# Second products in seven block products, in two parts that are combined in place in PSUM

## The chip, the core and the metric

The program runs on one core of one Trainium2 chip. The time is device microseconds of one execution of the whole program. The kernel before takes 1732.32 us, the median of three runs (1731.59 to 1733.02).

## The reference

512 tokens of width 1024 go through two blocks, all in float32. What matters here are three products that end a feed-forward stage, each with the weight's rows as the dimension that is summed over:

```python
def swiglu(x, w_in, w_out):                       # in the first block, twice; w_out is 2816 x 1024
    gate, up = jnp.split(x @ w_in, 2, axis=-1)
    return (jax.nn.silu(gate) * up) @ w_out
# first_block, each of its two layers, behind differential or chunked attention:
    x = layer_norm(DEEPNORM_ALPHA * x + swiglu(x, ffn_w_in[l], ffn_w_out[l]), ln_g[l, 1], ln_b[l, 1])
# second_block, behind its mixer of spatial gating and gated linear attention; w_ff2 is 4096 x 1024:
    f = rmsnorm(h, pre_ff_g[l]) @ w_ff1[l]
    f = jnp.square(jax.nn.relu(f)) @ w_ff2[l]
    h = h + rmsnorm(f, post_ff_g[l])
```

The two `ffn` are called the first and the second ffn here; the product with `w_ff2` is the last product of the program.

## The kernel before

**A product in three passes.** Each float32 operand is split into a high part (`hi`, the value rounded to the matmul's type) and a low part (`lo`, the value minus `hi`). A product is the sum of hi by hi, hi by lo and lo by hi in PSUM, so each block of it costs three matmuls.

**Weights.** The class `Weights` brings the weights in, in the order of their use, as a list of units. A raw tile of 128 x 1024 (512 KB) is loaded from the SP queue into one of three buffers (`wraw`), or, for some, into a lent tile (`room`). ACT then copies it into `whi` (line 127), and DVE subtracts that from it into `wlo` (line 130). There are five buffers of such pairs, and a unit's split is issued when the unit five places ahead of it is released by its last matmul (`fill`, called by `done`). A raw buffer is loaded anew as soon as it has been read.

**First products.** The first product of an ffn (1024 by 5632) and of the last stage already goes, for most column pairs, by a seven-product scheme for two-by-two blocks (`Blocks`). It needs sums of weights on DVE (lines 104 to 113), and its PSUM banks are emptied by DVE additions (lines 530 to 535), followed by the product of gate and up (line 827). In this stage the SP queue loads 512 KB for a weight tile, and DVE does three or four kinds of work beside PE.

**Second products.** These are the three that change. `Out` is one such product, `out_phase` its loops. The activations h stand as tiles k of 128 rows (22 in an ffn, 32 in the last product), which are split when they are first used (lines 786 and 787, into `th`, `tl` or, in the last product, `sh`, `sl`). Eight PSUM banks hold the result: four token tiles t of 128 by two halves c of 512 columns. Per k and t six matmuls of 512 columns run (line 387):

```python
            for n, (a, b) in enumerate(((0, 0), (0, 1), (1, 0))):
                for c in halves:
                    nc.tensor.matmul(self.banks[t][c], act[a][:, ts(t)], w[b][:, 0, c * 512:(c + 1) * 512],
                                     start=first and n == 0, stop=last and n == 2)
```

One k for four t is thus 24 matmuls. All k but the last six, seven or four (the tail) run over all t; the tail then runs token tile by token tile, so that the normalisation behind it begins early. At places given by `SPARE` an ffn splits a unit further ahead into a free tile of h.

**Order.** The program is written as one stream, and a scheduler sets each engine's own order from the dependences and its estimate of times; the SP queue keeps the order in which loads are written. An engine works through its list in that order, so an instruction that waits holds up all behind it.

## Time and profile before

| | |
|---|---|
| median of three runs | 1732.32 us |
| profiled execution | 1732.78 us |
| its span | 1731.1 us |
| mean granted clock of TensorE over the span | 0.998 of full speed |
| PE busy | 1716.9 us, 99% |
| DVE busy | 1213.4 us, 70% |
| ACT busy | 874.1 us, 50% |
| POOL busy | 128.6 us, 7% |
| moved by DMA | 191.62 MB, mean 111 GB/s |

The span runs from the first to the last instruction; the execution's own time stands 1.7 us above it. Busy time is an engine's time inside instructions; PE's matmuls overlap, so that the time from one start to the next, and not the length of one, is what a matmul costs. The rows below come from the same execution.

### The profile page before, as it was taken

The numbers are of one execution on the slowest core, as the hardware profiler recorded it, in microseconds if no ns is written. First come the engines' busy times: TensorE is split into PE (matmuls) and PEld (weight loads), VectorE is DVE, ScalarE is ACT, GpSimd is POOL, SyncE is SP. The second block draws the span as 40 slices with busy tenths as digits, with TensorE's granted clock in tenths as the row PEclk, the third lists the DMA queues.
The fourth block names the chain that finished last, engine by engine and source line by source line (L and its number), as shares of the span: only waits on it lengthen the run. The fifth ranks groups of instructions, "written<-read, shape, count | busy, mean of one in ns | idle before, by whom it ended". The sixth has DMA issues, their size and how long they took to land.

```text
span 1731.1 us, 27660 instructions
## 1 busy us (share of the span) xinstructions
PE 1716.9 (99%) x10886; PEld 1539.1 (89%) x10886; DVE 1213.4 (70%) x2056; ACT 874.1 (50%) x1458; POOL 128.6 (7%) x237
## 2 busy tenths in 40 slices
PE   9999999999999999999999999999999999999998
PEld 9888889999988888888999999888877899988886
DVE  6988868999943666666889998446646588953333
ACT  6877635444533377776544445333525356642221
POOL 0312102000000111220000000001001100000000
PEclk9999999999999999999999999999999999999999
DMA  6644346343443255552334344331422224343331
GB/s 208 136 99 110 98 146 185 110 115 105 123 133 122 73 114 136 123 140 81 98 91 118 102 114 154 110 87 50 123 72 87 80 73 124 108 134 98 97 98 49
DMA packets 207203, 191.62 MB, mean 111 GB/s; under 512 B 8800, under 2 KB 176928, under 8 KB 207072
## 3 DMA queue, kind: packets, MB, share of 16 engines
q1 hardware_dynamic: 194384, 162.48, 32.0%
q0 software_dynamic: 12112, 25.52, 6.7%
q8 instruction: 86, 1.41, 0.3%
q10 hardware_dynamic: 576, 1.84, 0.3%
q14 instruction: 45, 0.37, 0.1%
HBM read 172.99 MB, written 7.38 MB: 104 GB/s over the span
## 4 chain that ended last, share of the span: by engine, by line
PE 90%; DVE 3%; issue 3%; ACT 2%; POOL 1%; DMA 0%; ACTq 0%; POOLq 0%; DVEq 0%
PE ps L297 53%; PE ps L387 30%; PE ps L928 1%; PE ps L916 1%; PE ps L315 1%; PE ps L598 1%; PE ps L599 1%; ACT x L643 1%; DVE wlo L130 0%; ACT whi L127 0%; PE ps L704 0%; PE ps L728 0%; POOL ln_st L292 0%; DMA kl<-low 0%; PE ps L1128 0%
## 5 line engine op out<-in xcount | busy, mean ns | idle before, releaser
L127 ACT ACTIVATE whi<-wraw 128x1024 fp32r<-128x1024 f32 (+2 forms) x338 | 339.5, 1007 | 294.6 <-PE ps L297 162.3
L130 DVE TENSOR_TENSOR wlo<-wraw,whi 128x1024 fp32r<-128x1024 f32 (+2 forms) x338 | 390.5, 1159 | 105.9 <-ACT whi L127 102.9
L297 PE MATMUL ps<-xh,whi 128*128 128x256 f32 (+1 forms) x1220 | 379.4, 312 | 0.3 <-ACT xh L317 0.3
L297 PE MATMUL ps<-xl,whi 128*128 128x256 f32 (+1 forms) x1220 | 377.7, 310 | 0.5 <-DVE xl L318 0.3
L297 PE MATMUL ps<-xh,wlo 128*128 128x256 f32 (+1 forms) x1220 | 377.5, 310 | 0.0
L297 PEld LDWEIGHTS ps<-xh,wlo 128*128 128x128 f32 x1220 | 232.5, 191 | 11.2
L297 PEld LDWEIGHTS ps<-xl,whi 128*128 128x128 f32 x1220 | 232.5, 191 | 10.7 <-DVE xl L318 0.9
L297 PEld LDWEIGHTS ps<-xh,whi 128*128 128x128 f32 x1220 | 232.0, 191 | 10.7 <-ACT xh L317 0.5
L297 PE MATMUL ps<-th,whi 128*128 128x256 f32 x784 | 217.5, 277 | 0.0
L297 PE MATMUL ps<-tl,whi 128*128 128x256 f32 x784 | 217.1, 277 | 0.0
L297 PE MATMUL ps<-th,wlo 128*128 128x256 f32 x784 | 216.7, 276 | 0.0
L297 PEld LDWEIGHTS ps<-th,whi 128*128 128x128 f32 x784 | 147.6, 188 | 0.1
L297 PEld LDWEIGHTS ps<-tl,whi 128*128 128x128 f32 x784 | 147.6, 188 | 0.1
L297 PEld LDWEIGHTS ps<-th,wlo 128*128 128x128 f32 x784 | 147.3, 188 | 0.0
L297 PE MATMUL ps<-whi,xh 128*128 128x256 f32 (+1 forms) x384 | 124.4, 324 | 0.0
L297 PE MATMUL ps<-whi,xl 128*128 128x256 f32 (+1 forms) x384 | 122.5, 319 | 0.0
L297 PE MATMUL ps<-wlo,xh 128*128 128x256 f32 (+1 forms) x384 | 122.5, 319 | 0.0
L387 PE MATMUL ps<-whi,th 128*128 128x512 f32 x312 | 96.5, 390 | 0.0
L387 PE MATMUL ps<-whi,tl 128*128 128x512 f32 x312 | 96.1, 389 | 0.0
L387 PE MATMUL ps<-wlo,th 128*128 128x512 f32 x312 | 96.0, 389 | 0.0
L292 POOL TENSOR_TENSOR ln_st<-rs_in,mhalf 128x1 f32<-128x1 f32 x39 | 27.4, 702 | 821.6 <-DVE rs_in L291 814.6
L787 DVE TENSOR_TENSOR tl<-h,th 128x512 fp32r<-128x512 f32 x44 | 29.9, 690 | 79.4 <-ACT th L786 79.4
(350 smaller groups left out, 3164.8 us busy)
## 6 DMA issues: line engine op xcount, KB each, us to landing
wraw<-in_ffn_w_in SPq DMA_DIRECT2D x73, 512.0 KB, 4.7
wraw<-in_w_ff SPq DMA_DIRECT2D x60, 512.0 KB, 4.0
wraw<-in_ffn_w_out SPq DMA_DIRECT2D x44, 512.0 KB, 3.7
wraw<-in_a_w_qkv SPq DMA_DIRECT2D x23, 512.0 KB, 4.9
wraw<-in_w_in SPq DMA_DIRECT2D x20, 512.0 KB, 3.7
wraw<-in_kv_w SPq DMA_DIRECT2D x16, 512.0 KB, 4.1
room<-in_ffn_w_in SPq DMA_DIRECT2D x15, 512.0 KB, 4.0
copies<-extd POOLq DMA_DIRECT2D x16, 320.0 KB, 8.6
```

The lines of the kernel that those rows point to most:

```text
L127: self.nc.scalar.activation(hi[:, sl], t[:, sl], AF.Copy)
L130: self.nc.vector.tensor_tensor(lo[:, sl], t[:, sl], hi[:, sl].bitcast(F32), op=OP.subtract)
L292: nc.gpsimd.tensor_tensor(r, u[:, :n], mhalf[:, :n], op=OP.pow)
L297: nc.tensor.matmul(ps, lhs[a][lsel], rhs[b][rsel], start=first and n == 0, stop=last and n == 2)
L315: nc.tensor.transpose(p[:, k, :], y[:, ts(4 * c + k)], ident)
L387: nc.tensor.matmul(self.banks[t][c], act[a][:, ts(t)], w[b][:, 0, c * 512:(c + 1) * 512], start=first and n == 0, stop=last and n == 2)
L598: yield lambda: nc.tensor.matmul(p[:, :N], part[m][:, ts(i)], part[2 + m][:, :N], start=True, stop=False)
L599: yield lambda: nc.tensor.matmul(p[:, :N], part[m][:, ts(i)], part[4 + m][:, :N], start=False, stop=True)
L643: nc.scalar.activation(qs[32 * g:32 * g + 32], p[32 * (g ^ 1):32 * (g ^ 1) + 32], AF.Copy)
L787: nc.vector.tensor_tensor(lo, src[k], hi.bitcast(F32), op=OP.subtract)
L916: nc.tensor.transpose(p[:, j], e[:, ts(j)], ident)
L928: nc.tensor.matmul(p[:, q0:], v, aT[q][:, kt, q0:], start=kt == 0 and q == 0, stop=kt == NT - 1 and q == 1)
```

## The change

The contracted tiles of a second product are taken in pairs q, as two-by-two blocks: the even tile of weights is (B11 B12), the odd one (B21 B22), each block 512 columns; the activations' blocks A11, A12 belong to the first 256 tokens and A21, A22 to the last 256. Seven block products take the place of eight, for the first eight pairs of each ffn (`TWOF`) and twelve pairs of the last product (`TWO`). Each block product is two token tiles in three passes, 6 matmuls of 512 columns, so a pair has 42 in place of 48.

With S1 = A21 + A22, S2 = S1 - A11, S3 = A11 - A21, S4 = A12 - S2 and T1 = B12 - B11, T2 = B22 - T1, T3 = B22 - B12, T4 = B21 - T2 (the code works with its negative where that saves an operation):

- First part, for all pairs of the product in turn: S1·T1, S2·T2 (weights of the unit a0), A11·B11, S3·T3 (unit a1). Each goes into its own two banks, over all pairs.
- Between the parts the eight banks are combined once. ACT copies the banks of A11·B11 and of S1·T1 to SBUF after the last A11; DVE then adds S2·T2 to the copy of A11·B11 (line 547 of the changed kernel), and, in place in PSUM, adds this sum to the bank of S1·T1 (line 555) and to that of S3·T3 (line 557), and the copy of S1·T1 to that, into the bank of S2·T2 (line 558).
- Second part, again for all pairs: A12·B21, S4·B22 (unit b0) and A22·T4 (unit b1), added to the banks. Before A22·T4 its banks must have gone through lines 557 and 558, before S4·B22 its bank through line 555. A22·T4 goes into one half of columns only, the first.

After the last pair of the second part the banks hold the plain product of all pairs. The remaining tiles (6 in an ffn, 8 in the last product) run as before. In the last product the order after the first part is: pairs 0 to 2, tiles 24 and 25, pairs 3 to 5, tiles 26 and 27, pairs 6 to 11, and tiles 28 to 31 as tail.

**Weights.** Both tiles of a pair are needed in both parts, so they are loaded twice; in the first part only B22 of the odd tile (256 KB). The odd tiles go into lent buffers: in an ffn two in turn (`e1`, which is a tile named `e1` or, in the second ffn, `y`, and `room`), in the last product three in turn (two `y` and half of `gb`). DVE forms T1, T2, T3 from the raw tiles (lines 103 to 105) or T4 (lines 112 to 114). The low part of some units is not DVE's any more: for them ACT writes the negative high part into `lo` (the raw tile times -1, rounded), and a DMA issued by POOL adds the raw tile to it; these are the `added` units, a0 of the pairs with q not divisible by 4, and b0 of the pairs with q = 1, 4, 7, 10. In all other units line 157 does what line 130 did.

**Activations.** They are summed for two pairs at a time (lines 503, 504, 505 and 511, of 512 columns each), and split on ACT and DVE (line 494) into `th`, `tl` for the first two pairs of an ffn, else into eight places of 512 columns in `xh`, `xl`, which hold the ffn's input until its first product ends.

The diff, cut to its core:

```diff
+TWO, TWOF = 12, 8
...
+        while self.loaded <= i + (part not in (None, 0, "b0")):
             self.load()
+        tt = self.nc.vector.tensor_tensor
+        if part in ("a0", "b1"):
+            (e0, e1), (o0, o1) = ((t[:, :512], t[:, 512:]) for t in (self.r[i + (part == "b1")], self.r[i + (part == "a0")]))
+        if part == "a0":
+            tt(o0, e1, e0, op=OP.subtract)
+            tt(e1, o1, e1, op=OP.subtract)
+            tt(o1, o1, o0, op=OP.subtract)
+            return self._used(i + 1)[:, :], None
+        if part == "a1":
+            return self._used(i)[:, :], None
+        if part == "b0":
+            return self.r[i][:, :], None
+        if part == "b1":
+            tt(e1, e1, e0, op=OP.subtract)
+            tt(e1, e1, o1, op=OP.subtract)
+            tt(e0, o0, e1, op=OP.add)
+            self._used(i)
+            return self._used(i + 1)[:, :512], None
         if part is None:
             return self._used(i)[:, :], None
         if part == 0:
...
                 self.nc.scalar.activation(hi[:, sl], t[:, sl], AF.Copy)
                 if between:
                     between()
+                if self.split in self.added:
+                    self.nc.scalar.activation(lo[:, sl], t[:, sl], AF.Copy, scale=-1.0)
+                    self.nc.gpsimd.dma_start(lo[:, sl], t[:, sl], accum_op=OP.add)
+                    continue
                 self.nc.vector.tensor_tensor(lo[:, sl], t[:, sl], hi[:, sl].bitcast(F32), op=OP.subtract)
...
+    def spec_two(key, w, q, kind, transfer, group):
+        for n in range(2):
+            at[key, kind, q, n] = len(units)
+            if n in transfer:
+                added.add(len(units))
+            units.append((len(specs), kind + str(n)))
+        for odd in (0, 1) if kind == "a" else (1, 0):
+            c = 512 if kind == "a" and odd else 0
+            if odd and (kind == "b" or q > 1):
+                lent[len(specs)] = group
+            specs.append((cols(w, 256 * q + 128 * odd, 1, c, 1024 - c), (1, 1024 - c), None, c))
     wqkv = ins["a_w_qkv"]
...
+        w = ins["ffn_w_out"][l]
+        for q in range(TWOF):
+            spec_two(("fo", l), w, q, "a", (0,) if q % 4 else (), 2 + l)
+        for q in range(TWOF):
+            spec_two(("fo", l), w, q, "b", (0,) if q % 3 == 1 else (), 2 + l)
+        for k in range(2 * TWOF, 22):
+            spec((("fo", l), k), w, 128 * k, 1, 0, D)
...
-    rows("f2", ins["w_ff2_2"], 32)
+    w = ins["w_ff2_2"]
+    for q in range(TWO):
+        spec_two("f2", w, q, "a", (0,) if q % 4 else (), 4)
+    second = []
+    for q in range(TWO):
+        second.append(("b", q))
+        spec_two("f2", w, q, "b", (0,) if q % 3 == 1 else (), 4)
+        if q % 3 == 2 and 2 * TWO + 2 * (q // 3) + 2 <= 28:
+            for k in range(2 * TWO + 2 * (q // 3), 2 * TWO + 2 * (q // 3) + 2):
+                second.append(("one", k))
+                spec(("f2", k), w, 128 * k, 1, 0, D)
+    tail_f2 = [k for k in range(2 * TWO, 32) if ("one", k) not in second]
+    for k in tail_f2:
+        spec(("f2", k), w, 128 * k, 1, 0, D)
...
+    def two_parts(o, key, n_two, second, view, slots, tmp, z5, side={}):
...
+        def split(b, name, v):
+            hi, lo = slots(b, name)
+            nc.scalar.activation(hi, v, AF.Copy)
+            tt(lo, v, hi.bitcast(F32), op=OP.subtract)
+            parts[b, name] = hi, lo
+        def blocks(b):
+            v = view(b)
+            return [v[:, :, tile, half] for half in range(2) for tile in range(2)]
+        def sums(b):
+            (a11, a12, a21, a22), (s1, s2) = blocks(b), tmp
+            tt(s1, a21, a22, op=OP.add)
+            tt(s2, s1, a11, op=OP.subtract)
+            tt(a21, a11, a21, op=OP.subtract)
+        def splits(b):
+            (a11, a12, a21, a22), (s1, s2) = blocks(b), tmp
+            for name, v in (("S1", s1), ("S2", s2), ("A11", a11), ("S3", a21)):
+                split(b, name, v)
+            tt(a11, a12, s2, op=OP.subtract)
+        def first(b):
+            sums(b)
+            splits(b)
+        def then(b):
+            a11, a12, a21, a22 = blocks(b)
+            split(b, "A12", a12)
+            split(b, "S4", a11)
+            split(b, "A22", a22)
+        def product(unit, half, q, name, t0, c, begin):
+            w, act = W.get(at[unit]), parts[q // 2, name]
+            for m in range(2):
+                for n, (i, j) in enumerate(((0, 0), (0, 1), (1, 0))):
+                    nc.tensor.matmul(o.banks[t0 + m][c], act[i][:, q % 2, ts(m)], w[j][:, 4 * half:4 * half + 4],
+                                     start=begin and n == 0, stop=False, skip_group_check=True)
+        u = [t.rearrange("p a b -> p (a b)") for t in tmp]
+        def part_a():
+            for t in range(NT):
+                o.banks[t] = [bank(), bank()]
+            for q in range(n_two):
+                if q % 2 == 0 and q + 2 < n_two:
+                    first(q // 2 + 1)
+                product((key, "a", q, 0), 0, q, "S1", 0, 1, q == 0)
+                product((key, "a", q, 0), 1, q, "S2", 2, 1, q == 0)
+                W.done(at[key, "a", q, 0])
+                product((key, "a", q, 1), 0, q, "A11", 0, 0, q == 0)
+                if q == n_two - 1:
+                    then(0)
+                    for m in range(2):
+                        nc.scalar.activation(z5[:, m], o.banks[m][1], AF.Copy)
+                        nc.scalar.activation(u[m], o.banks[m][0], AF.Copy)
+                        tt(u[m], o.banks[2 + m][1], u[m], op=OP.add)
+                product((key, "a", q, 1), 1, q, "S3", 2, 0, q == 0)
+                W.done(at[key, "a", q, 1])
+        yield lambda: sums(0)
+        yield lambda: splits(0)
+        part_a()
+        for m in range(2):
+            tt(o.banks[m][1], o.banks[m][1], u[m], op=OP.add)
+        for m in range(2):
+            tt(o.banks[2 + m][0], o.banks[2 + m][0], u[m], op=OP.add)
+            tt(o.banks[2 + m][1], o.banks[2 + m][0], z5[:, m], op=OP.add)
+        for kind, q in second:
+            for f in side.get(q, ()) if kind == "b" else ():
+                f()
+            if kind == "one":
+                for t in range(NT):
+                    o(q, t)
+                o.done(q)
+                continue
+            if q % 2 == 0 and q + 2 < n_two:
+                then(q // 2 + 1)
+            product((key, "b", q, 0), 0, q, "A12", 0, 0, False)
+            product((key, "b", q, 0), 1, q, "S4", 0, 1, False)
+            W.done(at[key, "b", q, 0])
+            product((key, "b", q, 1), 0, q, "A22", 2, 0, False)
+            W.done(at[key, "b", q, 1])
...
+                o = Out(("fo", l), range(2 * TWOF, 22), splitter(lambda k: at_t(k - 2 * TWOF, 16), h))
+                halves = lambda t: t.rearrange("p (q s) -> p q s", q=2)
+                extra, lend = [hp.tile([128, D], F32, name=f"e{n}", bufs=1) if l == 0 else yp_[0].tile([128, D], F32, name="y")
+                               for n in range(2)], []
+                def lender():
+                    lend.append((extra[1], room)[len(lend) % 2])
+                    return lend[-1]
+                W.lender[1 + l] = lender
+                turn = []
...
+                def slots(b, name):
+                    if b == 0 and name in ("S1", "S2", "A11", "S3"):
+                        return [halves(t) for t in at_t(("S1", "S2", "A11", "S3").index(name), 0)]
+                    turn.append(name)
+                    return [halves(t[:, len(turn) % 8]) for t in (xh, xl)]
...
+                two = two_parts(o, ("fo", l), TWOF, [("b", q) for q in range(TWOF)],
+                                lambda b: four[b].rearrange("p (q e f s) -> p q e f s", q=2, e=2, f=2), slots,
+                                [halves(extra[0][:, n * S:n * S + S]) for n in range(2)],
+                                four[5][:, 2 * S:].rearrange("p (a b) -> p a b", a=2),
+                                {0: [norm_parts], 5: [spare], 6: [spare], TWOF - 1: [inner]})
+                first_sums, first_parts = next(two), next(two)
...
+                side = side_steps(then, 0, 2)
+                side[39] = [first_sums]
+                in_tiles(keys, evac, 4, tails, fast, side)
+                for f in two:
+                    f()
+                out_phase(o, finish, after, 22 - 2 * TWOF)
```

On DVE, at the end of the first ffn's first product: in both kernels the last block of that product is emptied from `ps` into `gb` (four instructions), with other work between. Before:

```order
L530 TENSOR_TENSOR gb_100<-ps_5289,gb_100 128x2x256
L787 TENSOR_TENSOR tl_2796<-h4_2786,th_2795 128x512
L531 TENSOR_TENSOR gb_100<-ps_5290,gb_100 128x512
L130 TENSOR_TENSOR wlo_5404<-wraw_5309,whi_5403 128x1024
L532 TENSOR_TENSOR gb_100<-ps_5290,gb_100 128x256
L535 TENSOR_TENSOR gb_100<-ps_5291,gb_100 128x512
L787 TENSOR_TENSOR tl_2796<-h4_2786,th_2795 128x512
L787 TENSOR_TENSOR tl_2796<-h4_2787,th_2795 128x512
L827 TENSOR_TENSOR h4_2791<-gb_100 128x512
L787 TENSOR_TENSOR tl_2796<-h4_2787,th_2795 128x512 x2
L130 TENSOR_TENSOR wlo_5447<-wraw_5340,whi_5446 128x1024
```

After; here `e0` holds sums of activations, `e1` and `wraw` are the raw tiles of a pair, and h4 are the activations:

```order
L690 TENSOR_TENSOR gb_100<-ps_5297,gb_100 128x2x256
L103 TENSOR_TENSOR e1_2799<-wraw_5317 128x512
L691 TENSOR_TENSOR gb_100<-ps_5298,gb_100 128x512
L157 TENSOR_TENSOR wlo_5390<-wraw_5256,whi_5389 128x1024
L692 TENSOR_TENSOR gb_100<-ps_5298,gb_100 128x256
L104 TENSOR_TENSOR wraw_5317<-e1_2799,wraw_5317 128x512
L695 TENSOR_TENSOR gb_100<-ps_5299,gb_100 128x512
L105 TENSOR_TENSOR e1_2799<-e1_2799 128x512
L503 TENSOR_TENSOR e0_2798<-h4_2787 128x512
L1019 TENSOR_TENSOR h4_2791<-gb_100 128x512
L504 TENSOR_TENSOR e0_2798<-e0_2798,h4_2787 128x512
L505 TENSOR_TENSOR h4_2787<-h4_2787 128x2x256
```

Between the four instructions now stand the sums of weights and of the next two pairs' activations where splits of activations (line 787) stood.

On DVE, further on in the same product, where the changed kernel passes from the first to the second part. Before, only two kinds of instruction alternate there:

```order
L787 TENSOR_TENSOR tl_2796<-h4_2788,th_2795 128x512
L130 TENSOR_TENSOR wlo_5477<-wraw_5374,whi_5476 128x1024
L787 TENSOR_TENSOR tl_2796<-h4_2788,th_2795 128x512
L130 TENSOR_TENSOR wlo_5509<-wraw_5407,whi_5508 128x1024
L787 TENSOR_TENSOR tl_2796<-h4_2788,th_2795 128x512
L130 TENSOR_TENSOR wlo_5541<-wraw_5450,whi_5540 128x1024
L787 TENSOR_TENSOR tl_2796<-h4_2788,th_2795 128x512
L130 TENSOR_TENSOR wlo_5573<-wraw_5480,whi_5572 128x1024
```

After; `e0` holds the sums for the combination, a half of `h4` the copy of S1·T1, and `ps` are the banks:

```order
L547 TENSOR_TENSOR e0_2798<-ps_5439,e0_2798 128x512
L547 TENSOR_TENSOR e0_2798<-ps_5441,e0_2798 128x512
L555 TENSOR_TENSOR ps_5435<-ps_5435,e0_2798 128x512
L555 TENSOR_TENSOR ps_5437<-ps_5437,e0_2798 128x512
L112 TENSOR_TENSOR wraw_5670<-wraw_5670 128x512
L557 TENSOR_TENSOR ps_5438<-ps_5438,e0_2798 128x512
L113 TENSOR_TENSOR wraw_5670<-wraw_5670,room_2797 128x512
L558 TENSOR_TENSOR ps_5439<-ps_5438,h4_2791 128x512
L114 TENSOR_TENSOR wraw_5670<-room_2797,wraw_5670 128x512
L557 TENSOR_TENSOR ps_5440<-ps_5440,e0_2798 128x512
L494 TENSOR_TENSOR xl_81<-h4_2787,xh_80 128x512
L157 TENSOR_TENSOR wlo_5759<-wraw_5670,whi_5758 128x512
```

The additions into the banks are interleaved with the sums and low parts of the second part's weights (lines 112 to 157) and with splits of activations (line 494).

On the SP queue, the loads of the first ffn's second weight. Before, one tile after the other into `wraw`:

```order
L81 DMA wraw_5132<-in_ffn_w_out 128x1024
L81 DMA wraw_5221<-in_ffn_w_out 128x1024
L81 DMA wraw_5251<-in_ffn_w_out 128x1024
L81 DMA wraw_5284<-in_ffn_w_out 128x1024
L81 DMA wraw_5309<-in_ffn_w_out 128x1024
L81 DMA wraw_5340<-in_ffn_w_out 128x1024
```

After:

```order
L84 DMA wraw_5256<-in_ffn_w_out 128x1024
L84 DMA wraw_5292<-in_ffn_w_out 128x512
L84 DMA wraw_5317<-in_ffn_w_out 128x1024
L84 DMA e1_2799<-in_ffn_w_out 128x512
L84 DMA wraw_5353<-in_ffn_w_out 128x1024
L84 DMA room_2797<-in_ffn_w_out 128x512
L84 DMA wraw_5393<-in_ffn_w_out 128x1024
L84 DMA e1_2799<-in_ffn_w_out 128x512
L84 DMA wraw_5470<-in_ffn_w_out 128x1024
L84 DMA room_2797<-in_ffn_w_out 128x512
```

Each pair is now a whole and a half tile, and the half ones go in turn into `e1` and `room`.

## Rows read from the trace of the kernel before

**Rows 1.** The page: busy us and share of the span by engine; DVE's tenths in 40 slices.

```profile
...
PE 1716.9 (99%) x10886; PEld 1539.1 (89%) x10886; DVE 1213.4 (70%) x2056; ACT 874.1 (50%) x1458; POOL 128.6 (7%) x237
...
DVE  6988868999943666666889998446646588953333
...
```

**Rows 2.** Chain of waits, whole span, longest pieces: start us, length us, what.

```profile
...
474.93 107.47 PE ps L387 x474
...
1550.26 157.55 PE ps L387 x695
...
```

**Rows 3.** Timeline of PE, first ffn's second product: start us, length, instruction xcount.

```profile
...
489.75 0.62 PE L387 MATMUL ps<-whi,th 128*128 128x512 f32 x2
...
492.02 0.62 PE L387 MATMUL ps<-whi,tl 128*128 128x512 f32 x2
...
```

**Rows 4.** Timeline of ACT there; in brackets the idle time before and its releaser.

```profile
...
485.48 0.63 ACT L786 ACTIVATE th<-h 128x512 fp32r<-128x512 f32 x1 [3.86 <-PE ps L387]
...
486.01 1.04 ACT L127 ACTIVATE whi<-wraw 128x1024 fp32r<-128x1024 f32 x1
...
490.92 0.63 ACT L786 ACTIVATE th<-h 128x512 fp32r<-128x512 f32 x1 [3.86 <-PE ps L387]
...
```

**Rows 5.** Timeline of DVE near the end of the first ffn's first product.

```profile
447.34 0.68 DVE L535 TENSOR_TENSOR h<-ps,gb 128x512 f32<-128x512 f32 x1
447.94 0.68 DVE L104 TENSOR_TENSOR room<-room 128x512 f32<-128x512 f32 x1
448.54 1.22 DVE L130 TENSOR_TENSOR wlo<-wraw,whi 128x1024 fp32r<-128x1024 f32 x1
449.67 0.69 DVE L827 TENSOR_TENSOR h<-h 128x512 f32<-128x512 f32 x1
450.27 0.69 DVE L105 TENSOR_TENSOR room<-wraw,room 128x512 f32<-128x512 f32 x1
450.99 0.69 DVE L108 TENSOR_TENSOR wraw<-room,wraw 128x512 f32<-128x512 f32 x1
```

**Rows 6.** Busy us (x instructions) by stretch: PE, PEld, DVE, ACT, POOL; clock, DMA.

```profile
...
475.00:483.00 8.00, 8.00 (x37) 6.62 (x36) 8.00 (x13) 4.37 (x7) 0.00 (x0) 1.00 0.65 202
...
530.00:540.00 10.00, 10.00 (x46) 8.28 (x45) 6.01 (x6) 4.30 (x6) 0.00 (x0) 1.00 0.47 154
...
1530.00:1540.00 10.00, 10.00 (x46) 8.28 (x45) 6.03 (x9) 5.12 (x7) 0.00 (x0) 1.00 0.45 141
...
```

**Rows 7.** Timeline of DVE: first instruction that empties the last two blocks' banks.

```profile
...
464.60 0.68 DVE L530 TENSOR_TENSOR h<-ps,h 128x512 f32<-128x512 f32 x1
...
474.78 0.68 DVE L530 TENSOR_TENSOR gb<-ps,gb 128x512 f32<-128x512 f32 x1
...
```

**Rows 8.** DMA issues: out<-in engine op xcount, KB each, median us to landing.

```profile
...
wraw<-in_ffn_w_out SPq DMA_DIRECT2D x44, 512.0 KB, 3.7
...
copies<-extd POOLq DMA_DIRECT2D x16, 320.0 KB, 8.6
...
bias<-copies POOLq DMA_DIRECT2D x16, 256.0 KB, 3.8
...
qk<-gb POOLq DMA_DIRECT2D x28, 128.0 KB, 4.9
...
x<-in_x SPq DMA_DIRECT2D x4, 256.0 KB, 4.1
...
```

**Rows 9.** Timeline of PE behind the second ffn, with the wait before.

```profile
...
1201.05 1.06 PE L315 MATMUL ps<-ident,y 128*128 128x128 f32 x8 [1.97 <-DVE y L967]
...
```

**Rows 10.** Two stretches right behind it, columns as in the windows above (PEclk).

```profile
...
1202.00:1204.00 2.00, 2.00 (x14) 2.00 (x13) 1.29 (x2) 0.80 (x2) 0.00 (x0) 0.58 0.00 0
...
1204.00:1206.00 2.00, 2.00 (x12) 2.00 (x12) 0.00 (x0) 0.00 (x0) 0.00 (x0) 0.57 0.00 0
...
```

**Rows 11.** Timeline of DVE at the last block before the last product.

```profile
...
1527.85 0.68 DVE L530 TENSOR_TENSOR gb<-ps,gb 128x512 f32<-128x512 f32 x1
...
```

**Rows 12.** Timeline of PE: first matmul of the last product.

```profile
...
1550.10 0.62 PE L387 MATMUL ps<-whi,sh 128*128 128x512 f32 x2
...
```

## What the change is expected to do

> **What bounds the kernel now.** I read the page's busy times and its slices first, then the chain of waits, then the timelines and windows of the three products that are changed. TensorE (PE) is busy 99% of the span, at full clock; VectorE (DVE) 70%, but unevenly: it sits at nine tenths in the stages of the first products and at three to six tenths in the second ones [rows 1]. The chain that ends last runs through the second products as one piece of matmuls each [rows 2]. So removing matmuls there shortens the kernel, as long as nobody else becomes late.
>
> A matmul of 512 columns costs 0.227 us: ten of them start between the two rows of [rows 3]. One tile of 128 rows of the second weight is 24 of them, 5.44 us, which is also the distance between two operand splits [rows 4].
>
> DVE has a price that is not its busy time. In the first products' stage an instruction of 512 columns lasts 0.68 or 0.69 us, but the next starts 0.60 after it; one of 1024 columns lasts 1.22 and the next starts 1.13 after it; where one needs the result of the one just before, the distance is 0.72 [rows 5]. I use 0.60, 1.13 and +0.12 for such a dependence.
>
> The Trainium skill speaks against this (VectorE: DVE Perf Modes, "The TRN2 errata" and "The DRAIN you can't avoid"): a 512-element fp32 tensor_tensor takes 691 ns, and the next does not start until the pipe is empty. The durations of [rows 5] agree with its 691, the starts do not agree with its drain; the rival below shows what it would make of the sum.
>
> **What goes.** A tile pair was 48 matmuls and becomes 42: six fewer, 1.36 us. Eight pairs in each ffn are 10.9 us, twelve in the last product 16.3 us; all together 168 matmuls, 38.1 us.
>
> **What comes to DVE.** Per pair in the first part: three sums of weights, 1024 columns of low parts for the second unit (for the first unit only in one pair of four, else ScalarE (ACT) and an adding DMA do it), and per two pairs eight instructions on activations. That is 3 x 0.65 + 1.13 + 0.3 + 2.5 = 5.9 us beside 5.44 us of PE. Before, the same two tiles cost it 2 x (1.13 + 0.60) = 3.5 us of 10.9; it has room in the stage, as has ACT [rows 6], but not that much, and not at its start.
>
> **Each ffn, first part.** In the first ffn DVE begins to empty the last block of the first product at 474.78, and the block before at 464.60 [rows 7]. In the changed order 14 instructions of 512, two of 1024 and one of 256 stand between these two: 8.4 + 2.3 + 0.3 + 0.6 for dependences = 11.6, so 476.2; two half tiles whose loads must wait for raw buffers can add up to 3. I take 478.0. From there to the second of the two additions into PSUM (line 555) stand 64 of 512, nine of 1024 and one of 256: 38.4 + 10.2 + 0.3 + 1.2 = 50.1, end 528.1. PE, starting at 474.9 [rows 2], has 8 x 5.44 + 1.36 = 44.9 us until it needs that addition (product S4), 519.8. DVE is 8.4 us late, whatever else happens. Ten more instructions, one of 1024, stand before the last addition (line 558) that product A22 needs for its second half: 6.7, at 534.8, against 521.7 without waits. So 13.1 us are lost against 10.9 won: +2.2 per ffn by DVE's list alone.
>
> Two tiles lent in turn add to this. Pairs 3, 5 and 7 share one: load, three sums (with those of the neighbour 3.2 us), two ACT passes (1.04 each [rows 4]), and an adding DMA that must land before the tile is loaded anew. The load is between 3.7 and 4.1; the add moves 512 KB inside SBUF, which no row shows. Nearest are 128 KB inside SBUF (4.9, queued four deep), 256 KB (3.8) and 320 KB (8.6) issued by POOL [rows 8]. I take 5.0, nearest to the copies inside SBUF; ends 3.8 and 8.6. A below-nothing end has no reason, as a wait can only come later. The link is 3.7 + 3.2 + 2.1 + 5.0 = 14.0 us, PE needs the tile every 10.9. The add of pair 3 lands about 22 us after DVE's start on the last block, that of pair 5 at 36, that of pair 7 near 49; then PE's first two products, A11 and ACT's copy put line 547 at 53 instead of 48: 5.4 more.
>
> The Trainium skill (Collectives: The Full Stack, "The bandwidth ceiling") says that an adding DMA costs by its two source reads, not by the add. By that this add would be as 1 MB of plain copy, an estimate of two loads, 7.4 us: 2.4 more at four places of each ffn, and the sum would be 1760; no run here shows it.
>
> **Second part.** 18 matmuls per pair, 4.08 us, beside about 4.5 us of DVE for some pairs and two loads of 512 KB instead of one and a half. The lent tile of pair 2 is free six instructions (3.6 us) after line 558; load 3.7, two passes 2.1, add 5.0 make 14.4, and PE wants pair 4 after 0.7 + 3 x 4.08 = 12.9: 1.5 late, with the other tile's DMA beside it up to 2.8. Upper end per ffn: 2.2 + 5.4 + 2.8 = +10.4. The lower end rests on DVE's pace alone; for the tile's turn each step but the add has its own row, so I take +8.0, nearer the upper end. The six single tiles after it cost DVE 1.7 of 5.44 us each and have their six operands split already: nothing.
>
> **The clock.** After PE had waited 1.97 us [rows 9], its granted clock was 0.58 and 0.57 for the next 4 us, most of it at 1.2 instead of 2.4 GHz [rows 10]: 1.7 us lost. A wait of several us at the start of each ffn's product should do the same once; I count 2 x 1.7. Later waits are for DVE or DMA, and a slow PE hides behind them.
>
> **The last product.** The stage before it is mild for DVE [rows 6]. From the last block at 1527.85 [rows 11] to the first line 547 stand 110 of 512, 16 of 1024, one of 256 and 25 dependences: 87.4, so 1615.3; up to 3 more, since the activations' new places (xh, xl) are read until 1550.1. PE starts the product at 1550.1 [rows 12] and reaches the end of A11 of pair 11 63.9 later, and ACT's copy 1.0 later: 1615.0. I take DVE 1.5 late. Eight more of 512 and one of 1024 (6.2) bring A22's second half to 1622.7 against 1618.8: 3.9 lost. Three lent tiles make the link 14.0 per 16.3 us, hidden. For six pairs in a row near the end I add 1.0. Net -16.3 + 4.9 = -11.4.
>
> **Sum.** 2 x 8.0 + 3.4 - 11.4 = +8.0 on the profiled execution's 1732.78, which stands 0.5 above the median of the runs: 1740.5 us.
>
> **Rivals.**
> 1. DVE's list is the only limit: loads and adds always land in time and the start is at 476.2. Then an ffn costs 2.2 - 1.8 = +0.4, no clock loss, the last product -12.4: 1721. For it: ACT and the DMA engines have room in these stages (DMA share 0.47 [rows 6]). Against it: two lent tiles, each reloaded only after an add. This ends on the faster side; it decides if the add lands in under 3 us.
> 2. The add lands as the 320 KB copies do, 8.6 us: 3.6 more at three links and once in the second part, +14.4 per ffn; the last product's link is then 17.6 per 16.3, +4. 1732.8 + 2 x 24.8 + 3.4 - 7.4 = 1778.
> 3. All 38.1 us are kept: 1694. For it only that PE is the whole chain now; against it the 50.1 us of DVE beside 44.9.
> 4. DVE pays its full duration each time, 0.09 more per instruction: 74 of them 6.7 per ffn, 127 of them 11 in the last product, +24: 1765. The starts of [rows 5] are against it. It is what the Trainium skill's drain (same page) would give.
>
> **Chances.** Forecast 0.46 (own range 1733 to 1752), first rival 0.22, second 0.13, third 0.03, fourth 0.03. The remaining 0.13 is a half-way case between forecast and first rival, lent tiles late by half, within 0.2% of before (3.5 us, about what a measurement of this kernel can tell from no change). Faster 0.25, same 0.13, slower 0.62. The range 1719 to 1764 holds the forecast, the first rival and the half-way case, and leaves out the other three rivals.
>
> **What would show it.** Right: PE's unbroken pieces of the two ffns break up; PE waits on DVE (lines 555, 558) at the change of parts and on the adding DMA or its low part in the first part; DVE near nine tenths there; the ffn products end about 8 us later relative to their start, the last one 11 earlier; the clock dips once in each ffn. Wrong: PE unbroken through the first part of an ffn, adds landing in 3 us, or DVE's list shorter than 50 us between the last block and line 555. A last product with waits before line 547 would break the term that carries the gain.

## The result and the profile after

The changed kernel takes 1759.7 us, the median of four runs (1759.37 to 1761.94), against 1732.37 for the kernel before beside it: a ratio of 1.0162, 95% interval 1.0150 to 1.0174. It is slower by 27.3 us where 8 were forecast. The direction held, and the time lies within 1719 to 1764, the range that takes in three outcomes; it lies outside 1733 to 1752, the forecast's own range.

The page, as in [rows 1]; then the chain of waits by engine:

```profile
PE 1697.7 (97%) x10718; PEld 1506.7 (86%) x10718; DVE 1395.7 (79%) x2371; ACT 974.6 (55%) x1599; POOL 154.7 (9%) x268
...
DVE  6888778999988666666889999967456589989774
...
PE 74%; DMA 9%; DVE 7%; issue 6%; ACT 3%; SPq 1%; POOL 0%; DVEq 0%; POOLq 0%; ACTq 0%
```

DVE's three to six tenths in the second products of [rows 1] have become eight or nine in the ffns' second products and in the first part of the last one, and the chain that was 90% PE now goes through DMA and DVE as well. PE's unbroken pieces [rows 2] are broken up; only behind the change of parts in the last product does PE run on without a wait. This is PE in the second part of the first ffn's product (line 527 issues the block products), with the wait before in brackets:

```profile
531.41 0.50 PE L527 MATMUL ps<-whi,xh 128*128 128x512 f32 x1 [0.21 <-DVE ps L555]
534.41 0.50 PE L527 MATMUL ps<-whi,xh 128*128 128x512 f32 x1 [0.41 <-DVE ps L558]
535.71 0.50 PE L527 MATMUL ps<-whi,xh 128*128 128x512 f32 x1 [0.33 <-ACT whi L149]
537.67 0.80 PE L527 MATMUL ps<-wlo,xh 128*128 128x512 f32 x1 [1.46 <-DMA wlo<-room]
553.20 0.73 PE L527 MATMUL ps<-whi,xh 128*128 128x512 f32 x2 [1.19 <-ACT whi L149]
555.07 0.50 PE L527 MATMUL ps<-wlo,xh 128*128 128x512 f32 x1 [1.14 <-DMA wlo<-e]
565.32 0.50 PE L527 MATMUL ps<-wlo,xh 128*128 128x512 f32 x1 [0.16 <-DVE wlo L157]
567.80 0.73 PE L527 MATMUL ps<-h,xh 128*128 128x512 f32 x2 [0.15 <-ACT h L149]
572.27 0.50 PE L527 MATMUL ps<-wlo,xh 128*128 128x512 f32 x1 [2.08 <-DMA wlo<-room]
574.44 0.62 PE L450 MATMUL ps<-whi,th 128*128 128x512 f32 x2
```

The change of parts (lines 555 and 558) costs almost nothing here. All three adds of the second part (`wlo<-room`, `wlo<-e`) are waited for. From the first S4 product (531.41) to the single tiles (574.44) are 43.0 us for 138 matmuls, 31.3 at 0.227; four matmuls of the single tiles, 0.9 us, stand among them.

In the last product one long wait stands at the change of parts. The chain that leads to it:

```profile
1636.83 6.43 DMA wlo<-y
...
1643.39 0.33 SPq L84
...
1643.81 6.96 DMA wraw<-in_w_ff
...
1650.79 0.70 DVE wraw L112
...
1654.14 1.21 DVE sums L547 x2
...
1655.37 0.71 DVE ps L555
```

PE and DVE there, from their timelines:

```profile
1656.13 0.80 PE L527 MATMUL ps<-whi,xh 128*128 128x512 f32 x1 [5.92 <-DVE ps L555]
1656.72 0.63 PE L527 MATMUL ps<-wlo,xh 128*128 128x512 f32 x1
1657.15 0.63 PE L527 MATMUL ps<-whi,xl 128*128 128x512 f32 x1
```

```profile
1638.23 0.69 DVE L112 TENSOR_TENSOR wraw<-wraw 128x512 f32<-128x512 f32 x1 [3.78 <-DMA wraw<-in_w_ff]
1638.84 0.69 DVE L494 TENSOR_TENSOR xl<-h,xh 128x512 fp32r<-128x512 f32 x1
...
1650.79 0.69 DVE L112 TENSOR_TENSOR wraw<-wraw 128x512 f32<-128x512 f32 x1 [2.98 <-DMA wraw<-in_w_ff]
```

An add holds a lent tile; SP's next load into that tile waits; the raw load behind it on SP starts 0.4 us after it and takes 6.96 us beside other traffic; DVE stands at the sum that needs it (line 112), and the additions into the banks stand behind that sum in DVE's list. PE waits 5.92 us and then runs at 0.43 us a matmul. Between waits DVE's starts are 0.60 us apart as in [rows 5].

Stage times used below: from the first to behind the last block product of each ffn ("two-part stage", 336 matmuls, 76.2 us at PE's pace; the same 16 tiles took 16 x 5.44 = 87.1 before), and from the last product's start to the end of the span (181.0 before, 1550.10 to 1731.1; 164.7 with all 16.3 us kept). The changed kernel has 100.7, 101.4 and 179.2: the ffns lose 13.6 and 14.3 us, the last product wins 1.8.

### The profile page after: what moved, and what is told of

Its sections match the earlier page's. It is cut to its first block, busy times and chain, and to the rows that moved or that the text cites. A ratio compares the mean times of both kernels' runs of the same rounds, so it can differ in the third digit from the quotient of the medians.

```text
span 1757.3 us, 28092 instructions
## 1 busy us (share of the span) xinstructions
PE 1697.7 (97%) x10718; PEld 1506.7 (86%) x10718; DVE 1395.7 (79%) x2371; ACT 974.6 (55%) x1599; POOL 154.7 (9%) x268
## 4 chain that ended last, share of the span: by engine, by line
PE 74%; DMA 9%; DVE 7%; issue 6%; ACT 3%; SPq 1%; POOL 0%; DVEq 0%; POOLq 0%; ACTq 0%
PE ps L360 50%; PE ps L450 13%; PE ps L527 4%; DMA wlo<-room 2%; DMA wraw<-in_ffn_w_out 2%; DVE wlo L157 1%; PE ps L1123 1%; ACT whi L149 1%; PE ps L1111 1%; PE ps L758 1%; PE ps L378 1%; PE ps L759 1%; ACT x L803 1%; DMA wraw<-in_w_ff 1%; DMA wlo<-y 1%
## 5 line engine op out<-in xcount | busy, mean ns | idle before, releaser
L157 DVE TENSOR_TENSOR wlo<-wraw,whi 128x1024 fp32r<-128x1024 f32 (+2 forms) x343 | 382.4, 1119 | 95.8 <-ACT whi L149 92.4
L360 PE MATMUL ps<-xh,whi 128*128 128x256 f32 (+1 forms) x1236 | 383.3, 311 | 0.0
L360 PE MATMUL ps<-xh,wlo 128*128 128x256 f32 (+1 forms) x1236 | 381.4, 309 | 0.0
L360 PEld LDWEIGHTS ps<-xl,whi 128*128 128x128 f32 x1236 | 234.9, 190 | 10.7 <-DVE xl L381 0.9
L527 PE MATMUL ps<-wlo,xh 128*128 128x512 f32 x340 | 139.7, 411 | 24.2 <-DMA wlo<-room 8.9
L527 PE MATMUL ps<-whi,xl 128*128 128x512 f32 x340 | 136.7, 402 | 0.0
L527 PE MATMUL ps<-whi,xh 128*128 128x512 f32 x340 | 122.6, 396 | 10.6 <-DVE ps L555 6.4
L527 PEld LDWEIGHTS ps<-wlo,xh 128*128 128x128 f32 x340 | 66.3, 195 | 47.9 <-DMA wlo<-room 12.0
L527 PEld LDWEIGHTS ps<-whi,xh 128*128 128x128 f32 x340 | 64.2, 190 | 28.6 <-DVE ps L555 7.6
```

What stands on the lines that cost most here:

```text
L157: self.nc.vector.tensor_tensor(lo[:, sl], t[:, sl], hi[:, sl].bitcast(F32), op=OP.subtract)
L360: nc.tensor.matmul(ps, lhs[a][lsel], rhs[b][rsel], start=first and n == 0, stop=last and n == 2)
L527: nc.tensor.matmul(o.banks[t0 + m][c], act[i][:, q % 2, ts(m)], w[j][:, 4 * half:4 * half + 4], start=begin and n == 0, stop=False, skip_g ...
```

## The experiments

Each time is a median, with its ratio to the kernel before run beside it and the 95% interval. Stages are the two ffns' and the last product's, as above, from the profiled execution.

One thing must be kept in mind with all of them. The scheduler sets the order of each engine's list anew for each kernel. In `norm_late` and `plain_copy` the lists of PE, DVE and ACT in the three products are those of the changed kernel, so their times show the edit alone. In `third_tile` and `skip_low` they are not, nor in `pool_low` and the runs without sums. DVE at the change of parts in the first ffn, in the changed kernel and in `skip_low` (lines are one lower there):

```profile
529.47 1.28 DVE L547 TENSOR_TENSOR e<-ps,e 128x512 f32<-128x512 f32 x2
530.67 1.29 DVE L555 TENSOR_TENSOR ps<-ps,e 128x512 f32<-128x512 f32 x2
```

```profile
521.94 0.68 DVE L546 TENSOR_TENSOR e<-ps,e 128x512 f32<-128x512 f32 x1
522.54 0.69 DVE L112 TENSOR_TENSOR wraw<-wraw 128x512 f32<-128x512 f32 x1
523.14 0.69 DVE L554 TENSOR_TENSOR ps<-ps,e 128x512 f32<-128x512 f32 x1
```

What such a run gains or loses is the edit together with the order that the scheduler makes around it.

**A third lent tile** (`third_tile`), and **the norm's loads moved alone** (`norm_late`):

```diff
-        self.room, self.n_pairs, self.lender = [n_raw, 1, 2, 2, 3], n_pairs, [None] * 4
+        self.room, self.n_pairs, self.lender = [n_raw, 1, 3, 3, 3], n_pairs, [None] * 4
-                    lend.append((extra[1], room)[len(lend) % 2])
+                    lend.append((extra[1], room, gb[:, 1])[len(lend) % 3])
-                                {0: [norm_parts], 5: [spare], 6: [spare], TWOF - 1: [inner]})
+                                {5: [spare], 6: [spare], TWOF - 1: [inner, norm_parts]})
```

The last two lines of the diff alone are `norm_late`.

> In each ffn the odd tiles go in turn into three lent tiles instead of two (the third is gb's second half), and the norm's two parameter loads, which use gb, move from the start of the second part to its end. Theory 1, the turn of two lent tiles (load, splits, adding DMA that lands 6.8 us after POOL takes it up, then the next load) is what PE waits for, with the raw loads held up behind it on SP's queue: the second part, which takes 43.0 us from its first S4 product in the first ffn, comes down to at most 36, the first part gives back about 5 of its 57.6, the whole program about 1735. Theory 2, the DMA engines are at their limit (about 260 GB/s in the second part with 1 MB for 18 matmuls): nothing but the 1 MB of the norm's parameters is won, 3.9 us in each ffn, 1752. Theory 3, DVE's list is the limit: no change, 1760.

> Only the norm's two parameter loads (1 MB) move from the start of each ffn's second part to its end; two lent tiles as in the changed kernel. Theory 1 (turn of the lent tiles): second parts shorter by at most 1 us each, 1758 to 1760. Theory 2 (DMA engines at their limit of about 260 GB/s): 3.9 us less in each ffn, 1752. Theory 3 (DVE): 1760.

Measured: 1774.4 (1.0251, 1.0236 to 1.0267), stages 106.6, 103.9, 180.0; and 1761.0 (1.0168, 1.0153 to 1.0183), stages 100.7, 102.1, 179.6. All three theories miss the first: it got slower. With one more tile the loads go out earlier (the fourth load of the first ffn's product is issued 9.2 us behind the product's start, before 17.6), and the adds land later. DMA issues of the adds to their landing, changed kernel, then third tile:

```profile
DMA to landing us min/median/max: 4.5/4.9/9.3
```

```profile
DMA to landing us min/median/max: 4.5/6.1/8.4
```

(The 6.8 us in the expectation misread the chain: POOL takes the add up 0.3 us behind ACT, and alone it lands 4.5 us later.) Moving 1 MB of loads from the start of the second part to its end changes nothing, as theories 1 and 3 had it, so the amount of loads there is not the limit by itself.

**No adding DMAs in the second part** (`b_no_add`: `transfer` is `()` for kind b), and **none at all** (`no_add`):

```diff
-    W.added = added
+    W.added = set()
```

> In the second part of all three products DVE makes all low parts; the adding DMAs stay in the first parts. Theory 1: the lent tile's turn loses 6.8 + 1.0 us of add and ACT and gains 1.1 of DVE three times in each ffn; each ffn's second part falls by about 6 us, 1748. Theory 2 (DMA engines): an add moves as much as one to two loads, three of them against sixteen loads, 4 to 6 us per ffn, the same 1748 to 1752. Theory 3 (DVE sets the second part): 3 x 1.1 us more in each, 1766.

> No adding DMA anywhere in the three products; DVE makes all low parts. Theory 1: the second parts fall by about 6 us each, while DVE's list in each ffn's first part grows by 6 x 1.13 = 6.8 us and becomes the limit there (first part 57.6 in the first ffn, then about 62), and the last product's grows by 10 and is late by 11 instead of the 10.8 of waits now: 1757. Theory 3 (DVE sets both parts already): 1759.7 + 2 x 10 + 10 = 1790. If the adds are the whole cause of the loss in the first part too, 1740.

Measured: 1752.6 (1.0122, 1.0107 to 1.0137), stages 99.5, 97.4, 174.6; and 1743.8 (1.0073, 1.0056 to 1.0090), stages 96.3, 95.7, 172.5. Giving the work back to DVE, the fuller engine, makes the kernel 16 us faster. The second run lies nearest to the 1740 of the adds as the whole cause; theories 1 and 3 (1757, 1790) miss it. Without adds DVE is the limit of both parts of an ffn; windows of the first ffn, columns as in [rows 6]:

```profile
474.00:533.00 59.00, 50.06 (x213) 38.22 (x212) 58.43 (x84) 33.28 (x50) 0.00 (x0) 1.00 0.41 134
533.00:570.00 37.00, 33.58 (x140) 25.36 (x139) 36.05 (x53) 14.40 (x19) 0.00 (x0) 1.00 0.61 214
```

**The two costs apart** (`skip_low`, `no_sums`):

```diff
 skip_low:
-                    self.nc.gpsimd.dma_start(lo[:, sl], t[:, sl], accum_op=OP.add)
 no_sums, on top of no_add:
-            tt(e1, o1, e1, op=OP.subtract)
-            tt(o1, o1, o0, op=OP.subtract)
...
-            tt(e1, e1, e0, op=OP.subtract)
-            tt(e1, e1, o1, op=OP.subtract)
```

> Leaves out the adding DMA itself and puts nothing in its place: the low part of those units stays what ACT writes, the negative high part, so the outputs differ. ACT's work, DVE's list, the loads and the order stay. Theory A, PE and DVE are both nearly full in these parts, and what an add holds back (its own unit, the lent tile, the raw load queued behind it on SP, DVE behind that load) is not made up again: the first parts fall from 58 to about 55, where DVE's list still sets the time, the second parts from 43 to 33, the last product's first part from 78.6 to about 69: 1759.7 - 2 x 13 - 10 = 1724. Theory B, the loads themselves are too slow (262 GB/s in the second part) with or without adds: second parts at 39 or more, 1742. Theory C, DVE alone: 1757.

> As the run without any adding DMA (1743.8), and two of the three sums of weights of each tile pair and part left out, so that the products are others. It takes 1.2 us per pair and part from DVE and nothing from any other engine. Theory A (without adds DVE is the limit of both parts of the ffns, 58.4 of 59.0 us busy in the first and 36.3 of 37.6 in the second): first parts from 58.5 to about 50, second parts from 37.5 to PE's own 31.5, last product's first part from 74.6 to about 68: 1743.8 - 2 x 14.5 - 6.5 = 1708. Theory B (loads): second parts stay at 37, first at 57, 1740.

Measured: 1716.8 (0.9912, 0.9898 to 0.9927), stages 85.4, 82.7, 165.2; and 1706.5 (0.9853, 0.9839 to 0.9868), stages 78.3, 77.7, 166.9. Theory A comes nearest in both (1724 and 1708). Without the adds, and in the scheduler's new order, the three stages are 15.3, 18.8 and 14.0 us shorter, 48 in all (the program 43; stages between them give some back). The other 9.2 and 6.5 us by which the ffns stand above PE's 76.2 are put down to DVE, as they go to 2.1 and 1.5 in `no_sums`, where DVE is relieved.

**POOL in place of the add** (`pool_low`):

```diff
-                    self.nc.scalar.activation(lo[:, sl], t[:, sl], AF.Copy, scale=-1.0)
-                    self.nc.gpsimd.dma_start(lo[:, sl], t[:, sl], accum_op=OP.add)
+                    self.nc.gpsimd.tensor_tensor(lo[:, sl], t[:, sl], hi[:, sl].bitcast(F32), op=OP.subtract)
```

> The low parts that the adding DMAs made are made by POOL, as a subtraction from SBUF to SBUF; ACT's negative copy and the DMA go. DVE's list stays. If POOL takes under 4 us for 1024 columns and leaves DVE at its pace, theory A gives what leaving out the adds gives, about 1726. If POOL takes 6 us or more, or DVE's distance of 0.60 us grows while POOL works, 1745 to 1760. Theory B (loads): 1742 or more.

Measured: 1806.8 (1.0440, 1.0423 to 1.0458), beyond every expectation. POOL's subtraction and a DVE instruction beside it, from the two timelines:

```profile
485.39 2.58 POOL L154 TENSOR_TENSOR wlo<-e,whi 128x1024 fp32r<-128x1024 f32 x1 [6.15 <-ACT whi L149]
496.84 7.52 POOL L154 TENSOR_TENSOR wlo<-room,whi 128x1024 fp32r<-128x1024 f32 x1 [8.87 <-ACT whi L149]
```

```profile
485.61 2.91 DVE L504 TENSOR_TENSOR h<-h 128x512 f32<-128x512 f32 x1
```

Over all 31 subtractions POOL takes 2.4 to 11.4 us. The DVE instruction that meets this one takes 2.91 us in place of 0.69; 24 DVE instructions that met one took 1.9 to 3.4.

**DVE relieved, adds kept** (`adds_no_sums`: the changed kernel with the four sums of `no_sums` left out), and then **the third lent tile with it** (`third_no_sums`):

> The changed kernel with all its adding DMAs, but two of the three sums of weights of each tile pair and part left out, so that the products are others; DVE has 1.2 us less per pair and part. Theory A1, an add is late only because DVE, which is nearly full, makes its sums late: with DVE relieved the adds land in time, two-part stages of about 79 us in each ffn (100.7 and 101.4 in the changed kernel, 78 in the run without adds and sums), the last product about 167: 1710. Theory A2, an add is late by itself (ACT's two passes, 0.3 and 4.5 to 9.3 us behind its sum, against 1.1 to 2.2 with DVE's low part), whatever DVE has to do: the adds go on costing what leaving them out gave, 14 to 19 us in each product, and only DVE's 9 us per ffn come back: 1759.7 - 18 = 1742.

> Leaves out two of the three sums of weights as before (so the products are others), keeps all adding DMAs, and gives each ffn the third lent tile. With DVE relieved the adds still cost 15 us in each ffn with two lent tiles (93.1 and 93.9 against 78.3 and 77.7) and 1 us in the last product with three. Theory T, the turn of the two lent tiles sets the ffns once DVE is out of the way: with three they fall to about 80 and 80, the program to 1719. Theory S, an add beside more loads gets slower (6.1 us median with three lent tiles against 4.9 with two) and its unit is late whatever the tiles: 92 or more, 1743 or more.

Measured: 1745.7 (1.0077, 1.0051 to 1.0102), stages 93.1, 93.9, 167.9; and 1740.6 (1.0058, 1.0041 to 1.0076), stages 91.3, 95.1, 174.9. Both spread more than the others (1740.2 to 1749.5 and 1739.1 to 1746.0), and the stages are those of the fastest and of the slowest execution, so a few us between these two say nothing. In the ffns the adds cost 15 and 16 us by themselves (against `no_sums`), as A2 had it. What they cost in the last product with DVE relieved is not settled: 1 us in the first run and 8 in the second, although the two kernels have the same instructions there in the same order on every engine; PE waits 1.5 us at the change of parts in the one and 6.2 in the other. The third tile does not mend the ffns, so Theory T falls. It moves the loss: the second part of the first ffn falls from 41.1 to 35.0 us, but the first part grows from 52.0 to 56.4, with one long wait at the change of parts, as in the last product of the changed kernel. PE, then DVE (lines are four lower: 551 is the changed kernel's 555, 110 its 114):

```profile
531.45 0.79 PE L523 MATMUL ps<-whi,xh 128*128 128x512 f32 x1 [7.35 <-DVE ps L551]
```

```profile
513.11 0.69 DVE L110 TENSOR_TENSOR wraw<-e,wraw 128x512 f32<-128x512 f32 x1 [4.94 <-DMA wraw<-in_ffn_w_out]
...
527.69 0.69 DVE L110 TENSOR_TENSOR wraw<-e,wraw 128x512 f32<-128x512 f32 x1 [2.58 <-DMA wraw<-in_ffn_w_out]
```

**A plain copy in place of the add** (`plain_copy`):

```diff
-                    self.nc.gpsimd.dma_start(lo[:, sl], t[:, sl], accum_op=OP.add)
+                    self.nc.gpsimd.dma_start(lo[:, sl], t[:, sl].bitcast(F32R))
```

> The adding DMA becomes a plain copy of the same 512 KB from the raw tile to the low part, without an add, so the outputs differ; order, waits and everything else stay. If an adding DMA costs as its source reads (two against one), a copy that stands alone takes about 2.3 to 3 us where the add took 4.49, each wait of PE on it is about 2 us shorter, and the program is at about 1740. If the add costs no more than the copy, 4.5 us again and 1760.

Measured: 1741.2 (1.0050, 1.0034 to 1.0066), stages 94.3, 92.7, 174.3. The copies to their landing:

```profile
DMA to landing us min/median/max: 2.9/3.4/6.6
```

Alone the copy takes 2.86 us; the add took 4.49, 1.57 times as much. All lists are in the same order here, so the 1.6 us per add are worth 18.5 us of the program, and 1740 was expected for this case. The Trainium skill (Collectives: The Full Stack, "The bandwidth ceiling") says of the add in a ReduceScatter that its two source reads make it slow and not the add itself; carried over to this add that would be two copies, 5.7, an estimate, and the measurement lies between one and two. The 1760 that the prediction gave by this rule comes so near the measured 1759.7 by chance: it rests on adds of 7.4 us in the ffns, and the 18 there took 4.5 to 5.6.

**Only the last product changed, without adds** (`last_no_add`: ffns as before), and three variants of it:

```diff
 last_two14:
-TWO, TWOF = 12, 8
+TWO, TWOF = 14, 8
 last_few_adds (last_five_adds: 2, 4, 6, 8, 10), with () for kind b:
-        spec_two("f2", w, q, "a", (0,) if q % 4 else (), 4)
+        spec_two("f2", w, q, "a", (0,) if q in (2, 4, 6) else (), 4)
```

> Both ffns as in the kernel before; the last product in two parts with twelve pairs, without adding DMAs. From the stages of the run without adds, the last product then takes 172.5 us where it took 181.0 before: 1731.2 - 8.5 = 1722.7, faster than both kernels. If the adds had been a help to DVE there, the last product takes as long as in the changed kernel, 179.2, and the whole 1729.4.

> As the run with only the last product changed and no adding DMAs (1722.5), with fourteen pairs instead of twelve. PE has 12 matmuls less, 2.7 us. DVE was 99% busy in that product's first part with 6.2 us per pair against PE's 5.44, so each pair more costs about what it saves: 1721 to 1725. If PE were the limit there: 1719.8.

> As the run with only the last product changed and no adding DMAs (1722.5), with three adds, for the odd tiles of pairs 2, 4 and 6 in the first part. DVE has 3.4 us less there, and no two adds stand side by side. If DVE is the limit and an add alone can be covered: 1720. If each add costs its own wait of 1 to 2.6 us on PE: 1723 to 1727.

> Only the last product changed, with five adds in its first part (pairs 2, 4, 6, 8, 10) where three gave 1719.8 and none 1722.5. If each add goes on saving DVE's 1.13 us: 1717.5. If PE has reached its own pace with three, or the later adds are late beside the loads for the second part: 1719.5 to 1722.

Measured: 1722.5 (0.9945, 0.9930 to 0.9960), 1727.6 (0.9973, 0.9962 to 0.9983), 1719.8 (0.9929, 0.9915 to 0.9944) and 1718.4 (0.9928, 0.9912 to 0.9945); the last product takes 171.7, 177.5, 168.3 and 167.0 us. Windows of its first part, without adds and with three:

```profile
1550.00:1624.00 74.00, 70.53 (x305) 56.50 (x304) 73.68 (x102) 42.06 (x59) 0.00 (x0) 1.00 0.47 151
```

```profile
1550.00:1624.00 74.00, 71.85 (x315) 58.59 (x314) 73.57 (x105) 45.50 (x63) 2.72 (x3) 1.00 0.59 176
```

The first came as expected (1722.7). DVE is full in both windows. Three adds are at most a small help: 2.7 us, and no execution of the one is as fast as the slowest of the other, but the intervals of the ratios overlap. From three to five nothing is shown, as the intervals overlap there too. All thirteen in the changed kernel were a harm (179.2 against 172.5 in `no_add`). Fourteen pairs cost 5 us more than twelve, outside the range expected: without single tiles between the pairs of the second part DVE is 97% busy there too. Three or five adds in the last product alone, with the ffns as before, beat the kernel before by 12 to 13 us and the changed one by 40.

## Why the prediction was wrong

**What held.** PE is the chain, and matmuls taken away are worth 0.227 each: `skip_low` has the last product at 165.2 of 164.7. DVE's pace of 0.60 and 1.13 held, and so its list: line 690 was forecast at 478.0, and the second line 555 to end 50.1 us later.

```profile
477.27 0.69 DVE L690 TENSOR_TENSOR gb<-ps,gb 128x512 f32<-128x512 f32 x1
...
530.67 1.29 DVE L555 TENSOR_TENSOR ps<-ps,e 128x512 f32<-128x512 f32 x2
```

That is 54.7 us, in 4.8 of which DVE waited for loads and for ACT. S4 was to come 8.4 us late by this list and up to 5.4 more by the lent tiles; it came 12.7 and 11.7 late (57.6 and 56.6 in place of 44.9). The price of one add held in the ffns: 4.5 us alone, 4.5 to 5.6 for the 18 there, against the 5.0 taken. The fourth rival falls by the starts of 0.60. The prediction takes the Trainium skill to speak against such starts, but the section that it names (VectorE: DVE Perf Modes, "The DRAIN you can't avoid") adds that a next instruction that is not held starts earlier; the trace agrees with that, with 0.60 us between starts where an instruction lasts 0.69. The first rival (adds always land in time, 1721) is what `skip_low` builds, 1716.8; its condition did not come about.

**What was luck.** No term of the sum gives the upper end of 1764 in which the time lies. And in the ffns a term that was too high made up for a part of one that was too low: DVE's list alone was to lose 13.1 us, and `skip_low` loses 9.2 and 6.5 in the order that it has; the lent tiles were taken at 5.8 (8.0 less 2.2), and without the adds the stages are 15.3 and 18.8 us shorter. So an ffn comes out only some 4 us beyond its forecast, 13.6 and 14.3 against 8.0 and the clock's 1.7. The last product has no such help and misses by 9.6 (1.8 won where 11.4 were forecast). (The sum, worked again, gives 1740.3 for the median and not 1740.5; nothing hangs on it.)

**What failed**, by size:

| term | forecast | measured |
|---|---|---|
| second part of each ffn, loss | 1.5 to 2.8 | 11.7 and 13.5 |
| last product, loss against 16.3 won | 4.9 | 14.4 |
| clock | 1.7 per ffn, none in the last | 3.4 per ffn, 2 in the last, within the rows above |
| behind the second ffn, up to the next stage | 0 | 3.4, of which 1.6 are left at the last product's start |

The first failing step is "The lent tile of pair 2 is free six instructions after line 558 ... 1.5 late". It priced one turn of one tile, once. Three things were left out of it. All eight pairs of the part bind, since DVE has no room there to make up a wait for a load (36.05 of 37 us busy without adds; with them 31.8 us of work beside PE's 31.3). An add is not only a link of the tile's turn but of its unit's own way to PE: ACT's second copy, 0.3 and 4.5 us stand where DVE's 1.13 stood, and PE waited to the landing of 12 of the 18 adds of the two ffns, 7.9 us in the first and 9.3 in the second. And each ffn lost 3.4 us to the clock behind such waits. That the adds slow the loads beside them does not show much here: the raw loads take a median 4.7 us in the first ffn, 4.4 in `skip_low`.

The second is "Three lent tiles make the link 14.0 per 16.3 us, hidden". The thirteen adds there took a median 6.2 us and up to 9.3 in place of 5.0, which makes the link 15.2 and up to 18.3; raw loads in the first part took a median 4.6 where `skip_low` has 3.7, and DVE waited 10.7 us for loads in the first part, 0.2 without adds. The wait came out at line 555, where the lists of DVE and SP put the combination behind a load.

The idea behind both steps, that a lent tile's turn is the add's price, is not borne out: a third tile cost 15 us with DVE full, and with DVE relieved it gave back nothing that stands clear of the spread. How much of the 48 us is the adds' own lateness, how much the loads they slow and how much the order that the scheduler makes around them stays open; with the order unchanged `plain_copy` shows that 1.6 us less in each gives back 18.5, which is nearly the whole miss of 19. What the adds cost in the last product with DVE relieved stays open too.

The clock did what [rows 9] and [rows 10] show, more often: after waits of 1.12, 1.46, 1.85 and 5.92 us the granted clock was 0.50 and matmuls stood 0.43 us apart, at 1.2 GHz, for some 3 us; after others, of 1.72, 2.08 and 2.75, it stayed at 2.4 GHz, so that the length of one wait does not tell. Behind the second ffn ACT waited for a late load of the next weight with the normalisation behind it in its list.

## What to carry to other kernels

That the DMA engines have room does not make it free to hand work from a full engine to a DMA: the transfer lengthens its own operand's way to the matmul, it can slow the loads beside it (in the last product here), and in-order lists pass the delay on. Price it at the moment when the consumer needs it, at every place and not at the worst one, and ask how full the engines are that would have to make up a wait. And judge a change per place: the same edit that loses 14 us in each ffn makes the program 12 us faster when it is made in the last product alone, with three of its thirteen adds.

## What the runs showed of the hardware

- A DMA of 512 KB inside SBUF took 2.86 us as a copy (`plain_copy`) and 4.49 as an add (the changed kernel) when nothing lay beside it, and up to 6.6 and 9.3 beside loads.
- A POOL subtraction of 1024 columns took 2.4 to 11.4 us, and DVE instructions that met one took 1.9 to 3.4 us in place of 0.69 or 1.22 (`pool_low`; spans on POOL are rough).
- DVE kept its 0.60 us between starts when 99% busy (`no_add`, first part of the first ffn).
- TensorE's granted clock fell to 0.50 after waits of 1.12 to 1.85 us in some places and not after waits of 1.72 to 2.75 in others.
